# A hybrid attention and state-space layer on one core: more transposes done by VectorE and transfers, panels and lags in a new order

## The chip, the cores and the metric

The kernel runs on one core of a Trainium2 chip. Its time is device microseconds from the start to the end of one execution. Engines are named as in the profile: PE is TensorE, DVE is VectorE, ACT is ScalarE, POOL is GpSimd, SP is SyncE, which issues most of the loads.

## The reference

One layer on 256 tokens of width 1024, in float32, with nine outputs of one combined input projection:

```
h  = RMSNorm(x)
[q|k|v|z|xBC|dt|g_a|g_b] = h @ W_in
y_a = softmax attention(RMSNorm(q), RMSNorm(k), v) @ W_o_attn        16 heads of 64, causal
y_b = RMSNorm_groups(ssd(conv(xBC), dt) * silu(z)) @ W_o_ssm        32 heads of 64, 4 groups, chunks of 128
x   = x + (sigmoid(g_a) * y_a + sigmoid(g_b) * y_b) @ W_out
x   = x + (silu(h2 @ W_g) * (h2 @ W_u)) @ W_down,  h2 = RMSNorm(x)
x   = x + (p @ W_ple_proj) * sigmoid(RMSNorm(x) @ W_ple_gate)
```

With 256 tokens the attention has one block, so it is plain causal attention. All weights are read once from DRAM, about 100 MB with the inputs, and every product is float32.

## The kernel before

**Products in parts.** A float32 product is made of three fp32r ones: each weight tile of 128 x 1024 (`raw`) is rounded by ACT to a high part `wh`, DVE subtracts (`wl` = `raw` - `wh`), and TensorE adds `wh` x high, `wh` x low and `wl` x high of the activations. Loads are issued by SP in the order of use, through 4 buffers `raw` and 5 each of `wh` and `wl`. `load_tiles` has a branch for tile numbers in `BY_DMA` that makes the low part without DVE; the set is empty here:

```
act(tiles[2], tiles[0], scale=-1.0)
nc.gpsimd.dma_start(tiles[2], src[:, k : k + 2], accum_op=ALU.add)
```

**Panels.** The projections are made in panels of 512 output columns, in the order of the table `PANELS`; its entries name q, k, v, z, xbc, the gates ga and gb, and the output products ya (attention) and yb (state space). A panel in *token form* has tokens on the PSUM partitions, and one product is 48 matmuls of 512 columns. In *rows form* (xbc and z, function `by_rows`) channels are on the partitions, and a matmul has 256 columns (the tokens); a panel in `WIDE` puts high and low of the tokens side by side, so that 32 matmuls have 512 columns and 32 have 256. Panels live in 4 PSUM banks `g`; 4 more, `pb`, take everything else.

**Small work between the panels.** Transposes, scores, values and the state-space pieces are generators of a `Filler`. It keeps a planned time of TensorE (`fill.now`) and lets a generator go on when the number of nanoseconds that it asked for in the table `LAG` has passed. So `LAG` and `PANELS` fix the order of TensorE, and manual dependencies (`queue`, `follow`) hold it. The other engines' order is made by a scheduler at build time from priorities. Every engine runs its list in order.

**Two ways to transpose.** By TensorE: `transpose` against an identity into a `pb` bank (128 x 128 each), then ACT and DVE take the high and low part out of the bank (`evac_qk`, `split_pair`). By transfers ("moved"): `turn` is a DVE transpose of 32 x 32 blocks, `put` writes it to DRAM by one DMA per 128 tokens, `get` reads it back in the block order by four DMAs, and ACT and DVE split what arrives (`split_moved`). Put and get are issued by POOL. `Sent` is a put that leaves half by half. The sets `MOVED_*` say which tiles go this way: in the kernel before the half m of the merged output (`MOVED_M`), the residual after W_out (`MOVED_R`) and some others.

**Attention.** `evac_qk` squares a panel (ACT), sums per head (DVE, line 777), scales and adds epsilon (DVE, 778), takes the power -0.5 (POOL, 780), and scales the bank into SBUF (DVE, 781). Then q and k are transposed and split (820). `scores` makes two heads' scores into two banks, masks, exponentiates and normalises them; `transp` transposes the probabilities for `values`.

**State space.** For each pair of heads POOL writes masked sums (`rr`, line 872, affine selects), which TensorE sums into decays; `rstd_of` takes a power on POOL (512, 513) for the groups' norm.

**Tail.** After the MLP, `Residual.take` (line 1418) adds each half of w_down to the residual; the first half is moved, the second (n = 1) is transposed by TensorE in `split_pair`, split by ACT and DVE (1189), and multiplied with the last weights; `final` scales, multiplies, adds and stores (1569 to 1571).

Of the kernel before, what the change touches and what calls it, by code (L numbers as in the profile page):

```python
# [38 lines left out]
    ('gb', 1, 9760),  # L39
    ('xbc', 1, 5632),  # L40
    ('xbc', 5, 7680),
# [26 lines left out]
def by_rows():  # L68
# [4 lines left out]
WIDE = [('xbc', 0), ('xbc', 2), ('xbc', 3), ('xbc', 4), ('xbc', 5), ('z', 1), ('z', 2)]  # L73
# [18 lines left out]
    "dt.low": [322],
    "dt.end": [300],
    "c.get": [6000, 6000, 6000, 6000, 6000, 6000],
    "z.get": [6000, 6000, 6000, 6000],
    "x.get": [6000, 6000, 6000, 6000],
    "qk.get": [6000, 6000, 6000, 6000],
    "c.moved": [11500, 14000, 14000, 14000, 22000, 25400],
    "c.rows": [0, 2000, 0, 825, 500, 500],
    "x.moved": [28600, 8500, 20160, 14000],  # L100
    "x.start": [0, 0, 0, 0],
    "x.end": [5000, 4125, 2550, 1850],
    "p.moved": [24000, 15200, 20200, 8500, 24000, 8500, 24000, 24000],
    "qk.moved": [55800, 20000, 20000, 20000],
    "qk.split": [4200, 2560, 0, 4000],
    "xbc.end": [500, 0, 8000, 5175, 6606, 13539],
    "z.turn": [1000, 1000, 5000, 2000],
    "z.moved": [10000, 8500, 8500, 15000],
    "z.end": [0, 3383, 0, 10000],
    "qk": [14924, 21622, 13695, 19850],  # L110
    "qk.turn": [30000, 20000, 3500, 10000],
    "qk.t": [0, 500, 4448, 3521, 677, 1338, 1217, 1187],
    "qk.end": [0, 3102, 0, 3764],
    "v": [4043, 1000],
    "cb": [17, 0, 1060, 0],
    "rows": [4315],
    "prep": [5212, 300, 3707, 2704, 2974, 1163, 928, 2558],
    "seg": [4750, 2800, 500, 0, 0, 0, 1550, 4500, 300, 0, 2336, 1000, 3310, 4661, 1000, 2000],
    "seg.next": [10101, 11100, 0, 12046, 14480, 2104, 11572],
    "out": [0, 12163, 4964, 6250],  # L120
    "out.xdt": [0, 10000, 300, 0],
    "out.end": [509, 705, 4450, 0],
    "off": [1878, 3935, 0, 5814],
    "off.end": [0, 2831, 1117, 0],
# [64 lines left out]
def tile_layer(ctx: ExitStack, tc: tile.TileContext, head, xk, pt, vec, w_dt, w_big, w_dn2, w_pp, out):  # L189
# [1466 lines left out]
```

## Time and profile before

| | |
|---|---|
| median of 3 runs | 579.67 us (579.21 to 579.83) |
| profiled execution | 580.19 us, span 578.5 us |
| granted TensorE clock | 1.00 |
| busy: PE, DVE, ACT, POOL | 572.3, 443.0, 333.7, 82.0 us |
| DMA engines | 113.88 MB, mean 197 GB/s |

A busy PE row counts overlapping matmuls, so the rate of TensorE is read from the distance of starts, not from the mean duration. The chain of waits names, for each piece of time, the work that what followed had to wait for.

### The profile page before, as it was taken

The page shows a single profiled execution, that of the slowest core. Times are in us where ns is not written, and L with a number is a line of the kernel's source. Part 1 is how long each engine was busy: PE and PEld are TensorE (multiplying, and loading weights), DVE is VectorE, ACT ScalarE, POOL GpSimd, SP SyncE. Part 2 cuts the span into 40 slices and gives each one's busy share as a digit, 9 for nine tenths or more (in the row PEclk, how much of TensorE's full clock was granted, in tenths as well). Part 3 has the DMA queues.
Part 4 walks back from the last instruction along what each step waited for, and adds up shares of the span by engine and source line. Part 5 has one row for each costly group of instructions (what it writes and reads, how often), then busy time and mean ns, then how long its engine had stood idle before and what let it go on. Part 6 is the DMA issues. An engine that isn't in the chain of part 4 may idle for free.

```text
span 578.5 us, 8580 instructions
## 1 busy us (share of the span) xinstructions
PE 572.3 (99%) x3077; PEld 483.2 (84%) x3077; DVE 443.0 (77%) x696; ACT 333.7 (58%) x526; POOL 82.0 (14%) x116
## 2 busy tenths in 40 slices
PE   9999999999999999999999999999999999999996
PEld 8887898898988888888887888888888888888885
DVE  6668899998799899999757586776767767655563
ACT  6856567765668658666763544645455455444542
POOL 2011220000422310100000200300312012202010
PEclk9999999999999999999999999999999999999999
DMA  8874655545344653545445886576887687858611
GB/s 314 322 253 141 211 170 172 179 138 192 130 152 140 205 166 124 170 128 182 149 144 177 269 270 190 167 252 219 267 270 241 228 256 240 256 199 238 217 65 73
DMA packets 36458, 113.88 MB, mean 197 GB/s; under 512 B 4576, under 2 KB 8000, under 8 KB 36416
## 3 DMA queue, kind: packets, MB, share of 16 engines
q1 hardware_dynamic: 33088, 104.03, 54.7%
q0 software_dynamic: 3040, 8.92, 5.3%
q8 instruction: 24, 0.39, 0.3%
q10 hardware_dynamic: 288, 0.39, 0.2%
q14 instruction: 18, 0.15, 0.1%
HBM read 107.74 MB, written 5.52 MB: 196 GB/s over the span
## 4 chain that ended last, share of the span: by engine, by line
PE 88%; DMA 4%; DVE 4%; POOL 1%; ACT 1%; issue 1%; SPq 0%; ACTq 0%
PE g L273 78%; PE pb L273 8%; PE pb L295 3%; DMA raw<-in_w_big 2%; DVE wl L375 2%; DMA raw<-in_head 2%; POOL tiny L780 1%; ACT wh L252 1%; DVE s L1345 1%; DVE tiny L777 0%; DVE s L1347 0%; SPq L349 0%; ACT s L252 0%; DVE s L820 0%; DVE s L781 0%
## 5 line engine op out<-in xcount | busy, mean ns | idle before, releaser
L273 PE MATMUL g<-wh,s 128*128 128x512 f32 (+1 forms) x1156 | 358.9, 389 | 0.1
L252 ACT ACTIVATE wh<-raw 128x1024 fp32r<-128x1024 f32 (+2 forms) x192 | 199.0, 1040 | 177.7 <-PE g L273 137.3
L375 DVE TENSOR_TENSOR wl<-raw,wh 128x1024 fp32r<-128x1024 f32 (+2 forms) x193 | 230.9, 1199 | 90.0 <-ACT wh L252 88.4
L273 PEld LDWEIGHTS g<-wh,s 128*128 128x128 f32 x1156 | 216.3, 188 | 44.7 <-issue 0.5
L273 PE MATMUL g<-wl,s 128*128 128x512 f32 (+1 forms) x578 | 223.2, 388 | 0.0
L273 PEld LDWEIGHTS g<-wl,s 128*128 128x128 f32 x578 | 108.4, 188 | 21.9 <-issue 0.2
L273 PE MATMUL g<-s,wh 128*128 128x512 f32 (+1 forms) x416 | 114.5, 347 | 0.7 <-DVE s L781 0.7
L273 PE MATMUL g<-s,wl 128*128 128x256 f32 x320 | 86.6, 283 | 0.0
L273 PEld LDWEIGHTS g<-s,wh 128*128 128x128 f32 x416 | 70.6, 190 | 8.7 <-ACT wh L252 1.1
L273 PEld LDWEIGHTS g<-s,wl 128*128 128x128 f32 x320 | 60.6, 190 | 2.8
L252 ACT ACTIVATE s<-s 128x512 f32<-128x512 f32 (+4 forms) x45 | 35.0, 785 | 14.1 <-DVE s L1016 4.3
L252 ACT ACTIVATE s<-pb 128x512 f32<-128x512 f32 (+3 forms) x51 | 23.4, 477 | 14.8 <-PE pb L273 9.0
L273 PE MATMUL pb<-s,s 128*64 128x128 f32 (+5 forms) x336 | 29.0, 294 | 0.0
L872 POOL TENSOR_SCALAR_AFFINE_SELECT rr<-a_h 128x512 fp32r<-128x512 f32 x16 | 13.5, 863 | 108.7 <-PE pb L273 85.0
L273 PEld LDWEIGHTS pb<-s,s 128*64 128x64 f32 (+2 forms) x336 | 23.6, 158 | 5.9 <-issue 3.1
L780 POOL TENSOR_TENSOR tiny<-tiny,mhalf 128x8 f32<-128x8 f32 x8 | 19.7, 2461 | 48.2 <-DVE tiny L778 48.2
L647 DVE SCALAR_TENSOR_TENSOR s<-s,vecs,s 128x255 f32<-128x255 f32 (+2 forms) x60 | 26.3, 470 | 0.0
L749 POOL DMA_DIRECT2D s<-turn_d x36 | 19.8, 557 | 39.0 <-DMA turn_d<-s 36.9
L741 POOL DMA_DIRECT2D turn_d<-s x14 | 10.7, 762 | 100.3 <-DVE s L731 100.3
L252 ACT ACTIVATE s<-s,vecs 128x256 f32<-128x256 f32 (+1 forms) x44 | 21.7, 544 | 2.3 <-DVE s L1378 2.3
L295 PE MATMUL pb<-ident,s 128*128 128x128 f32 x146 | 22.1, 272 | 0.0
L252 ACT ACTIVATE s<-g 128x256 f32<-128x256 f32 (+1 forms) x46 | 20.3, 455 | 1.7 <-PE g L273 1.7
(145 smaller groups left out, 371.0 us busy)
## 6 DMA issues: line engine op xcount, KB each, us to landing
raw<-in_w_big SPq DMA_DIRECT2D x176, 512.0 KB
turn_d<-s POOLq DMA_DIRECT2D x16, 256.0 KB, 4.8
s<-turn_d POOLq DMA_DIRECT2D x32, 128.0 KB, 5.4
raw<-in_head SPq DMA_DIRECT2D x4, 512.0 KB
s<-in_xk SPq DMA_DIRECT2D x4, 512.0 KB
raw<-in_head SPq DMA_DIRECT2D x6, 256.0 KB
s<-e_d SPq DMA_DIRECT2D x8, 128.0 KB
raw<-in_w_pp SPq DMA_DIRECT2D x2, 512.0 KB
```

What stands on the lines that cost most here:

```text
L252: return nc.scalar.activation(o, i, f, **kw)
L273: ins = nc.tensor.matmul(o, lhsT, rhs, start=start, stop=stop).ins
L295: queue(nc.tensor.transpose(o, i, ident[: i.shape[0], : i.shape[0]]).ins, main)
L375: nc.vector.tensor_sub(wl, raw, wh.bitcast(F32))
L647: stt(cc[j][:, sft:], pu[:, j, : T - sft], cw[j][3 - sft], cc[j][:, sft:], op0=ALU.mult, op1=ALU.add)
L741: nc.gpsimd.dma_start(d[:, :, at : at + t_.shape[2]].rearrange("b p n -> p b n"), t_)
L749: nc.gpsimd.dma_start(o[32 * b : 32 * b + 32], d[b].rearrange("(a i) n -> i a n", i=32))
L780: nc.gpsimd.tensor_tensor(f, ms, mhalf, op=ALU.pow)
L872: nc.gpsimd.affine_select(r, bcast(a_h[:, c, h0 : h0 + 4].bitcast(F32), P), pattern=[[0, 4], [1, P]], compare_op=ALU.is_ge, fill=0.0, base ...
L1345: stt(h32[:, j], xk_, g1[:, k + j : k + j + 1], pr, op0=ALU.mult, op1=ALU.mult)
```

## The change

- `MOVED_QK = {0}`: q and k of the first half (k0, q0) go by `turn`, `put` and `get` instead of 16 transposes on TensorE.
- `MOVED_P`: the probabilities of three head pairs go the same way instead of 18 transposes; ACT scales them instead of DVE.
- `MOVED_Z = {2, 3}`: the panels z2 (was wide rows form) and z3 (was rows form) are made in token form and turned afterwards.
- `MOVED_E = {1}`: the residual of the tail, second half, goes by DVE and transfers instead of 8 transposes; its put and get are issued by SP.
- `BY_DMA = {38, 46, 54, 64}`: the low parts of four weight tiles are made by ACT and an accumulating DMA of POOL.
- `PANELS`: xbc5 ahead of xbc1, z2 ahead of xbc3, ga1 earlier, yb2 in two halves, and the last panel before w_out is the second half of yb3 instead of ya1.
- `LAG` and `FLIP`: all numbers new.

```diff
--- before.py
+++ after.py
@@ PANELS
     ('gb', 1, 9760),
+    ('xbc', 5, 7680),
     ('xbc', 1, 5632),
-    ('xbc', 5, 7680),
...
+    ('z', 2, 4096),
     ('xbc', 3, 6656),
-    ('z', 2, 4096),
     ('yb', 1, None),
     ('v', 1, 2560),
-    ('yb', 2, None),
+    ('ga', 1, 8736),
     ('ga', 0, 8224),
+    ('yb', 2, 0),
     ('yb', 3, 0),
     ('ya', 0, None),
-    ('ga', 1, 8736),
+    ('yb', 2, 1),
+    ('ya', 1, None),
     ('yb', 3, 1),
-    ('ya', 1, None),
...
-WIDE = [('xbc', 0), ('xbc', 2), ('xbc', 3), ('xbc', 4), ('xbc', 5), ('z', 1), ('z', 2)]
+WIDE = [('xbc', 0), ('xbc', 2), ('xbc', 3), ('xbc', 4), ('xbc', 5), ('z', 1)]
...
-    "m.moved": [22000],
+    "m.moved": [8500, 18300],
...
-MOVED_QK = set()
+MOVED_QK = {0}
 MOVED_X = set()
-MOVED_Z = set()
+MOVED_Z = {2, 3}
 MOVED_C = set()
-MOVED_P = set()
-BY_DMA = set()
+MOVED_P = {(1, 1), (1, 2), (1, 3)}
+BY_DMA = {38, 46, 54, 64}
 MOVED_M = {0}
+MOVED_E = {1}
...
-    def get(d):
+    def get(d, on=None):
 
         o = s4([4, d.shape[2]])
         for b in range(4):
-            nc.gpsimd.dma_start(o[32 * b : 32 * b + 32], d[b].rearrange("(a i) n -> i a n", i=32))
+            (on or nc.gpsimd).dma_start(o[32 * b : 32 * b + 32], d[b].rearrange("(a i) n -> i a n", i=32))
         return o
...
-        def __init__(self):
+        def __init__(self, on=None):
             self.d = dram.tile([4, P, T], F32, name=nm("turn_d"))
+            self.on = on or nc.gpsimd
...
-            turned = get(d).rearrange("p a (t i j) -> p i t a j", t=2, i=4)
+            turned = get(d, sent and sent.on).rearrange("p a (t i j) -> p i t a j", t=2, i=4)
...
-            sent = Sent() if self.normed and n == 0 else None
+            sent = Sent() if self.normed and n == 0 else Sent(nc.sync) if not self.normed and n in MOVED_E else None
...
+                elif sent:
+                    fill.spawn(split_moved([b[:, 0], b[:, 1]], self.cols(n), self.acts[n], lag("res"), sent), 0)
```

The tables do not show what moves. At three places it is this.

VectorE around the scaling of the first half's q and k (`s_99` is the first 128 tokens of q, `pb_600` and `pb_610` hold the transposed k). Before:

```order
L777 TENSOR_REDUCE tiny_563<-s_98_560 128x8
L820 SCALAR_TENSOR_TENSOR s_115_599<-pb_600,vecs,s_114_598 128x4x128
L820 SCALAR_TENSOR_TENSOR s_115_599<-pb_610,vecs,s_114_598 128x4x128
L778 TENSOR_SCALAR tiny_563<-tiny_563,eps_207 128x8
L375 TENSOR_TENSOR wl_779<-raw_777,wh_778 128x1024
L781 TENSOR_TENSOR s_99_561<-g_475,tiny_566 128x512
```

Now:

```order
L780 TENSOR_REDUCE tiny_563<-s_98_560 128x8
L781 TENSOR_SCALAR tiny_563<-tiny_563,eps_207 128x8
L377 TENSOR_TENSOR wl_760<-raw_758,wh_759 128x1024
L784 TENSOR_TENSOR s_99_561<-g_475,tiny_566 128x512
L580 TENSOR_REDUCE tiny_dt_596<-pb_595 128x64
```

The two splits of the transposed k are gone from between q's reduction and its scaling; the turns of both panels come later in VectorE's list.

POOL where the second half's q takes its powers, among the selects of the state space (`rr`), in the changed kernel, with the gets of a panel and the first accumulating DMA (`wl_1697`) ahead of them:

```order
L751 DMA s_184_1027<-turn_d_849 32x4x256 x4
L395 DMA wl_1697<-in_w_big 128x1024
L875 AFFINE_SELECT rr_1714<-a_h 128x512
L875 AFFINE_SELECT rr_1718<-a_h 128x512
L783 TENSOR_TENSOR tiny_1635<-tiny_1632,mhalf 128x8
L875 AFFINE_SELECT rr_2036<-a_h 128x512
L875 AFFINE_SELECT rr_2040<-a_h 128x512
L783 TENSOR_TENSOR tiny_1644<-tiny_1641,mhalf 128x8
```

Before, the two powers stood together behind eight selects:

```order
L872 AFFINE_SELECT rr_1794<-a_h 128x512
L872 AFFINE_SELECT rr_1798<-a_h 128x512
L872 AFFINE_SELECT rr_2088<-a_h 128x512
L872 AFFINE_SELECT rr_2092<-a_h 128x512
L780 TENSOR_TENSOR tiny_1686<-tiny_1683,mhalf 128x8
L780 TENSOR_TENSOR tiny_1695<-tiny_1692,mhalf 128x8
```

A pair of selects now stands between the two powers, and gets and an accumulating DMA ahead of them.

SP at the end of the program, where the last weights (`raw`) are loaded and the outputs stored. Before:

```order
L389 DMA raw_5587<-in_w_big 128x1024
L389 DMA raw_5593<-in_w_big 128x1024
L1571 DMA out<-s_1098_5577 128x512
L1571 DMA out<-s_1099_5582 128x512
L1571 DMA out<-s_1106_5635 128x512
```

Now:

```order
L391 DMA raw_5560<-in_w_big 128x1024
L391 DMA raw_5566<-in_w_big 128x1024
L761 DMA turn_d_5383<-s_1079_5385 128x4x128
L761 DMA turn_d_5383<-s_1080_5389 128x4x128
L751 DMA s_1098_5426<-turn_d_5383 32x4x256 x4
L1576 DMA out<-s_1113_5550 128x512
```

The two puts and four gets of the residual's second half stand between the last weight load and the first store, so they pass no load and only the stores stand behind them.

More of the change, by code (lines that the diff above doesn't have):

```diff
@@ L88 @@
 LAG = {
-    "dt": [8019],
-    "dt.t": [9610],
+    "dt": [7695],
+    "dt.t": [1649],
     "dt.e": [44376],
[L92 to L124, printed above, removed]
@@ L125 @@
-    "finish": [305, 9922, 13731, 6496],
-    "finish.ones": [10000, 2521, 0, 12856],
-    "sc": [8201, 2775, 5000, 0, 6165, 5667, 15876, 3962],
-    "sc.tr": [7150, 3550, 8766, 10000, 0, 680, 852, 0],
-    "tr": [0, 5000, 0, 0, 2688, 8460, 0, 739],
-    "tr.val": [8261, 5950, 21961, 0],
-    "val.end": [237],
-    "m": [3541, 0],
+    "dt.low": [1420],
+    "dt.end": [7330],
+    "c.get": [4600, 20580, 4500, 10000, 7500, 6618],
+    "z.get": [4500, 4500, 4884, 33641],
+    "x.get": [8244, 12274, 13232, 6932],
@@ new lines @@
+    "qk.get": [12918, 8033, 4500, 10000],
+    "c.moved": [34125, 31752, 10992, 30743, 8500, 32731],
+    "c.rows": [1000, 1200, 570, 1250, 675, 2749],
+    "x.moved": [13995, 8500, 47462, 23039],
+    "x.start": [2900, 300, 8000, 5000],
+    "x.end": [13264, 5000, 400, 1000],
+    "p.moved": [15262, 8500, 8500, 8500, 8500, 8500, 8500, 20319],
+    "qk.moved": [10248, 8500, 27777, 8500],
+    "qk.split": [0, 0, 5180, 9250],
+    "xbc.end": [4179, 10000, 1800, 6195, 1009, 27735],
+    "z.turn": [4786, 1000, 2000, 300],
@@ new lines @@
+    "z.moved": [21550, 8500, 15232, 12790],
+    "z.end": [1608, 2533, 166, 10000],
+    "qk": [35463, 4100, 10000, 500],
+    "qk.turn": [36000, 14085, 3250, 573],
+    "qk.t": [9888, 20340, 801, 2717, 7875, 1154, 500, 2000],
+    "qk.end": [6850, 5592, 6870, 6500],
+    "v": [500, 6762],
+    "cb": [5146, 300, 5500, 1180],
+    "rows": [32],
+    "prep": [360, 1220, 3538, 10000, 6191, 5850, 4616, 0],
+    "seg": [786, 1000, 1733, 2000, 0, 2240, 675, 2200, 270, 0, 4657, 630, 6561, 1161, 300, 300],
@@ new lines @@
+    "seg.next": [13430, 1807, 0, 10763, 3340, 13729, 1598],
+    "out": [0, 12126, 0, 1796],
+    "out.xdt": [23394, 6500, 9891, 4930],
+    "out.end": [0, 1900, 0, 4911],
+    "off": [4846, 6856, 5500, 500],
+    "off.end": [0, 4316, 0, 0],
+    "finish": [12156, 12574, 10000, 0],
+    "finish.ones": [10000, 4145, 0, 5360],
+    "sc": [3858, 9680, 4744, 9313, 6576, 2190, 10631, 2078],
+    "sc.tr": [49, 8107, 2493, 0, 0, 18653, 29052, 2020],
+    "tr": [540, 14500, 11511, 7222, 8494, 0, 2000, 2000],
@@ L133 @@
+    "tr.val": [0, 1100, 0, 0],
+    "val.end": [0],
+    "m": [8091, 716],
     "res": [5337, 5987],
-    "m.moved": [22000],
+    "m.moved": [8500, 18300],
     "r.moved": [24000],
@@ L151 @@
 FLIP = {
-    "sc": [1, 0, 1, 0, 1, 0, 1, 0],
-    "out": [0, 0, 1, 0],
-    "val": [1, 1, 0, 0],
+    "sc": [0, 1, 0, 1, 0, 0, 0, 1],
+    "out": [0, 1, 0, 1],
+    "val": [0, 1, 0, 0],
 }
@@ L1233, in joined @@
         acc, ga = accs[n], gates["ga", n]
-        sent = Sent() if n in MOVED_M else None
+        sent = Sent(nc.scalar if n else None) if n in MOVED_M else None
         with prio("ev"):
@@ L1243, in joined @@
         if sent:
-            fill.spawn(split_moved(toks, None, m_act[n], lag_of("m.moved", 0), sent), 0)
+            fill.spawn(split_moved(toks, None, m_act[n], lag_of("m.moved", n), sent), 0)
         else:
```

2 lines of the change are left out of this document (1 added, 1 removed).

## The prediction

> **What bounds the kernel now.** I read the shares of the engines first, then the chain of work that ended last, then the groups of TensorE's instructions by shape. The first row is the page's; the others are the chain in order of time (start us, length us, what).
>
> ```profile
> PE 572.3 (99%) x3077; PEld 483.2 (84%) x3077; DVE 443.0 (77%) x696; ACT 333.7 (58%) x526; POOL 82.0 (14%) x116
> ```
>
> ```profile
> 57.49 0.60 DVE tiny L777
> 58.08 0.07 DVE s L820
> ...
> 58.66 0.74 DVE s L820
> 59.40 0.15 DVE tiny L778
> ...
> 59.62 2.56 POOL tiny L780
> 62.20 0.70 DVE s L781
> ...
> 63.04 12.11 PE g L273 x98
> ...
> 345.52 0.44 PE pb L295 x4
> ...
> 401.36 156.75 PE g L273 x693
> ...
> 562.89 9.62 PE g L273 x48
> 572.51 1.45 PE pb L273 x12
> ```
>
> Up to 62.90 us the chain runs through loads, splits and one VectorE-GpSimd exchange; from 63.04 us it is TensorE alone, each piece starting where the one before it ends, until 573.96. So after 63 us an instruction taken from TensorE is worth its whole pitch, as long as no new wait opens. DVE, ACT and POOL have room on average, so they matter only where something of theirs is due at a given moment.
>
> The pitch comes from the chain: 156.75 / 693 = 0.2262 us for a matmul of 512 columns, and 0.44 / 4 = 0.11 us for a 128x128 transpose. "Mean ns" of a group is longer, since matmuls overlap; it is not used. For the two other shapes I take TensorE's timeline, in which the distance of starts is the pitch:
>
> ```profile
> 69.10 0.28 PE L273 MATMUL g<-s,wl 128*128 128x256 f32 x1
> 69.22 0.40 PE L273 MATMUL g<-s,wh 128*128 128x256 f32 x2
> 69.46 0.28 PE L273 MATMUL g<-s,wl 128*128 128x256 f32 x1
> ...
> 100.57 0.40 PE L273 MATMUL g<-s,wh 128*128 128x512 f32 x1
> 100.81 0.28 PE L273 MATMUL g<-s,wl 128*128 128x256 f32 x1
> 100.92 0.40 PE L273 MATMUL g<-s,wh 128*128 128x512 f32 x1
> ```
>
> Three 256-column matmuls of the rows form take 0.36 us (69.10 to 69.46), 0.12 each; one wide pair of 512 and 256 takes 0.35 (100.57 to 100.92).
>
> **What TensorE loses.** The instruction lists differ by 42 transposes: 16 of q and k, 18 of three pairs of probabilities, 8 of the last residual's second half. 42 x 0.11 = **-4.6 us**. They stand among these:
>
> ```profile
> L295 PE MATMUL pb<-ident,s 128*128 128x128 f32 x146 | 22.1, 272 | 0.0
> ```
>
> z2 goes from 32 wide pairs to 48 matmuls of 512 columns: 32 x 0.35 = 11.2, 48 x 0.2262 = 10.9, so -0.3. z3 goes from 96 of 256 columns to the same 48: 11.5 - 10.9 = -0.7. Together **-1.0 us**. The other matmuls keep shape and number; reordered panels cost nothing by themselves.
>
> **The place before 63 us.** The chain's VectorE rows show two L820 operations (the low parts of k of the first half) between the reduction L777 and L778. They are gone there, and with them their 1.3 us (58.08 to 59.40). TensorE's own last start before its gap is this:
>
> ```profile
> 61.95 0.39 PE L273 MATMUL g<-wh,s 128*128 128x512 f32 x1
> ```
>
> One pitch later, at 62.18, it would have gone on; it starts at 63.04, so it stands 0.86. In the new order 8 transposes ahead of it are away (already counted), so it arrives at 61.3, and the power, now 1.3 earlier, has L781 done at 61.6 and TensorE started at about 61.75. The gap shrinks to 0.45: **-0.4 us**. At best it closes (-0.9), at worst another DVE operation fills the hole (0).
>
> **The exchanges, and what hides them.** Each moved tile costs VectorE a turn, GpSimd (or SP) a put and four gets, and two landings:
>
> ```profile
> L731 DVE STREAM_TRANSPOSE s<-s 128x512 f32<-128x512 f32 x16 | 11.2, 705 | 0.3
> ...
> L820 DVE SCALAR_TENSOR_TENSOR s<-pb,vecs,s 128x512 fp32r<-128x512 f32 x8 | 5.8, 739 | 0.0
> ```
>
> ```profile
> L749 POOL DMA_DIRECT2D s<-turn_d x36: 549/553/624, 324.4 to 531.2; - x36
> L741 POOL DMA_DIRECT2D turn_d<-s x14: 755/758/823, 403.8 to 523.5; - x14
> ...
> DMA to landing us min/median/max: 2.7/4.9/7.1
> ```
>
> POOL (GpSimd) gets 46 DMAs more, 14 puts x 0.76 + 28 gets x 0.55 + 4 accumulating loads priced like puts = 29.1 us on an engine of 82.0; VectorE gets 16 turns (about 10 us) and loses 4 L375 and 4 L820 and multiplications, about as much. Neither fills up. What counts is latency: put, landing, get, landing is 2 x 4.9 plus about 3 of issue, some 13 us. I laid the new order of TensorE on the clock with the pitches above and compared when each result is used. k and q of the first half arrive 10 us or more before the scores that read them; the probabilities of the third moved pair some 3 us before their values; m of the first half, whose gets were issued in this way,
>
> ```profile
> 314.93 0.98 POOL L758 DMA_DIRECT2D turn_d<-s  x1 [26.92 <-DVE s L731]
> 319.54 0.76 POOL L758 DMA_DIRECT2D turn_d<-s  x1 [3.62 <-DVE s L731]
> 324.36 2.20 POOL L749 DMA_DIRECT2D s<-turn_d  x4 [4.06 <-DMA turn_d<-s]
> ```
>
> is now due 21.8 us after its last panel instead of 27, and needs about 17: still 4 spare. These I cost at nothing; cover gone, each costs what its landing exceeds the spare by.
>
> Two places are tight. The power L780 for q of the second half now stands on GpSimd behind selects that wait for TensorE's own segment sums, so q's scaling is about 1 us later, while the panel's bank is wanted soon after: 0 to 1.4 us, I take **+0.4**. And m of the second half, by TensorE's transposes as before (those at 345.52), is used about 8 matmuls earlier: its low part takes one ACT and one DVE step, due after 0.5 to 1 us, 0 to 0.4, I take **+0.2**.
>
> **The tail.** Residual n=1 is turned and goes out and back on SP's queue instead of by 8 transposes.
>
> ```profile
> 550.51 1.28 DVE L1418 TENSOR_TENSOR s<-g,s 128x512 f32<-128x512 f32 x2
> ...
> 558.59 1.64 ACT L252 ACTIVATE s<-pb,vecs 128x256 fp32r<-128x256 f32 x4 [1.04 <-PE pb L295]
> ```
>
> ```profile
> 550.62 0.33 SPq L389 DMA_DIRECT2D raw<-in_w_big  x1
> 567.90 7.83 SPq L1571 DMA_DIRECT2D out<-s  x5
> ```
>
> In the clock of before the additions end at 551.79, two turns at 553.2, the second put is issued by 553.6. SP waits there for it, then issues four gets (0.33 each), with nothing queued behind but the outputs. TensorE wants the first result at 562.89 - 0.88 = 562.0. No row has this exchange on SP's queue. From above: the median landing of GpSimd's transfers, twice: 553.6 + 4.9 + 1.3 + 4.9 = 564.7, plus 0.5 for ACT's split: a stall of 3.2. From below: 2.7 twice gives 560.8: none. The stage is nearest to the lower end, since the traffic has thinned:
>
> ```profile
> 115.00:160.00 45.00, 45.00 (x325) 41.40 (x324) 38.09 (x79) 28.34 (x59) 7.09 (x6) 1.00 0.47 153
> ...
> 400.00:550.00 150.00, 150.00 (x663) 124.20 (x663) 100.13 (x110) 73.06 (x81) 26.00 (x42) 1.00 0.76 239
> 550.00:578.00 28.00, 23.94 (x133) 20.73 (x131) 14.13 (x21) 10.05 (x17) 2.26 (x6) 1.00 0.19 67
> ```
>
> The last columns are the DMA engines' share and GB/s: 0.19 instead of 0.76. I take landings of 3.2, ready at 561.8, and a DVE low part a little late: **+0.4**. ACT holds the last weight's rounding behind these splits, but TensorE reaches that weight 30 matmuls (6.8 us) later.
>
> [...]
>
> **Low parts by DMA.** For four weight tiles ACT writes the negated rounding and an accumulating DMA adds the weights. No row shows such a DMA. Its nearest row is the four gets above, also 512 KB together on GpSimd's queue: landing between 2.7 and 7.1 after issue. TensorE wants those low parts 6 to 8 us after the issue, so I cost it at 0; four times a landing at the upper end plus 1 would be a few us.
>
> **The sum.** The profiled execution took 580.19 us, of which the span is 578.5; the median is 579.67, 0.5 lower. -4.6 - 1.0 - 0.4 + 0.4 + 0.2 + 0.4 = -5.0, and 0.3 for small waits that I did not find: -4.7. 580.2 - 4.7 - 0.5 = **575.0 us**. With all bounds at their good ends it is 573.2, with the two tight places and the tail at their bad ends about 579.
>
> **Rivals.**
>
> *The tail waits.* With median landings the stall of 3.2 replaces 0.4: 577.8. For it: 4.9 is what a transfer of this trace usually took, and the last weights' loads still run beside the puts. Against: 0.19 traffic. Chance 0.12.
>
> *GpSimd's single file.* A get waits on GpSimd for its put's landing, and powers and selects that TensorE needs stand behind it. L780 shows how such a wait is passed on: VectorE idled 8.8 us ahead of its eight scalings for it.
>
> ```profile
> L781 DVE TENSOR_TENSOR s<-g,tiny 128x512 f32<-128x512 f32 x8 | 5.5, 691 | 8.8 <-POOL tiny L780 8.8
> ```
>
> ```profile
> POOL rr L872 <- PE pb L273: 85.0, 6, 64.8
> ...
> POOL s L749 <- DMA turn_d<-s: 36.9, 8, 5.3
> ```
>
> GpSimd stood 36.9 / 8 = 4.6 us per exchange, and there are seven new ones on GpSimd, the early ones among the selects. If three of them pass on 1.4 us each, 575.0 + 4.2 = 579.2: no change. Against: GpSimd now waits 85.0 us for TensorE at its selects, so it is mostly early there. Chance 0.12. [...]
>
> *The accumulating DMAs land late; slower.* They must read the tile, add and write it. If that takes twice the gets' median of 4.9, 9.8 us, against 7 of cover, each of four holds TensorE 2.8 us, in order: +11.2, 586. From a landing of 8.5 (1.5 late, 4 x 1.5 = 6) the kernel is slower than before. Against: the maximum of 7.1, and the moderate traffic where the first of them stands (0.47 at 115 to 160 us). Chance 0.10.
>
> **How the numbers follow.** The forecast's case (573.2 to 577) has 0.66, the rivals 0.12, 0.12, 0.10. The range, 573.3 to 579.6, takes in the first two rivals and leaves out the slower one and a tenth of no-change cases. A measurement of this kernel tells a change of 0.2%, 1.2 us, from none: faster (below 578.5) is the first two cases and a third of the single-file case, 0.81; same 0.08; slower 0.11.
>
> **What would show it.** TensorE's L295 group at 104 instead of 146, its span's gap near 62 us at half a microsecond, no gap over 0.3 us between 63 us and the tail, and DMA landings of about 3 us on the tail's exchange. A wait of TensorE on the low parts written by DMA, or on a select behind a get, would make the prediction wrong; so would a lower granted clock than the 1.00 in the windows above.

## The result, and the profile after

The changed kernel takes **576.08 us** (median of 6 runs, 575.73 to 576.63) against 579.77 us of the kernel before on the same chip: ratio 0.9932, interval 0.9919 to 0.9945. That is 3.7 us less; the forecast was 4.7 less (575.0). The profiled execution took 576.59 us, its span 574.9 instead of 578.5; the granted clock was 1.00 in the windows up to TensorE's tail, so the prediction's proviso on the clock did not come in.

First the shares and the group of transposes of the kernel after, from the page and from the groups by shape:

```profile
PE 568.3 (99%) x2971; PEld 475.8 (83%) x2971; DVE 443.3 (77%) x703; ACT 337.8 (59%) x531; POOL 109.7 (19%) x162
...
L297 PE MATMUL pb<-ident,s 128*128 128x128 f32 x104 | 15.2, 272 | 0.0
```

TensorE has 106 matmuls less and is as full as before. VectorE's busy time hardly moved, GpSimd's rose by 27.7 us (29.1 forecast). The chain of waits of the kernel after, as start, length, work:

```profile
58.77 13.11 PE g L275 x71
...
90.55 0.34 DVE s L1381
...
90.93 27.31 PE g L275 x179
...
549.43 4.53 DMA turn_d<-s
...
555.43 2.87 DMA s<-turn_d
...
558.96 9.92 PE g L275 x48
568.88 1.45 PE pb L275 x12
```

Before, one piece of TensorE followed another from 63.04 us to the end. Now the chain leaves TensorE twice: from 72 to 91 us it runs over VectorE (a chain that is followed back lists all that VectorE did without a pause, so these 19 us are not 19 us of waiting), and in the tail it runs over the new exchange. What TensorE lost there is seen in its timeline, in which the distance of two starts is compared with the usual pitch. The three places of the kernel after (start us, length us, instruction; in brackets idle time and what ended it):

```profile
61.61 0.39 PE L275 MATMUL g<-wh,s 128*128 128x512 f32 x1
61.84 0.44 PE L275 MATMUL g<-s,wh 128*128 128x512 f32 x1
...
90.06 0.39 PE L275 MATMUL g<-s,wh 128*128 128x512 f32 x1
90.93 0.50 PE L275 MATMUL g<-s,wh 128*128 128x512 f32 x1 [0.48 <-DVE s L1381]
...
558.13 0.28 PE L275 MATMUL pb<-wh,s 128*128 128x256 f32 x1
558.96 0.50 PE L275 MATMUL g<-wh,s 128*128 128x512 f32 x1 [0.56 <-ACT s L254]
```

At 61.61 there is no gap in this profile, where before 0.86 us were lost. At 90.06 the distance is 0.87 instead of 0.24: 0.63 us lost, at a place that had no gap before. At 558.13 it is 0.83 instead of 0.12, and the first matmul behind it takes 0.11 longer (558.96 to 559.30): 0.82 lost.

A fourth loss is spread over a few matmuls. m of the second half is still transposed by TensorE, and the matmuls that read it follow haltingly:

```profile
350.31 0.40 PE L275 MATMUL g<-wl,s 128*128 128x512 f32 x1
350.70 0.74 PE L275 MATMUL g<-wh,s 128*128 128x512 f32 x2
351.28 0.40 PE L275 MATMUL g<-wl,s 128*128 128x512 f32 x1
```

0.39 instead of 0.227, then 0.58 instead of 0.454 for two; with the matmul before and after them 0.44 us.

TensorE's last matmul ends at 570.33 instead of 573.96, 3.63 us earlier. By places, against the terms of the prediction:

| place | predicted us | measured us |
|---|---|---|
| 42 transposes | -4.6 | -4.58 |
| z2, z3 in token form | -1.0 | -0.98 |
| near 62 us | -0.4 | -0.32 |
| q1's power behind selects | +0.4 | 0 |
| m, second half | +0.2 | +0.44 |
| tail exchange | +0.4 | +0.82 |
| 90 us (L1381) | not listed | +0.63 |
| small waits | +0.3 | +0.36 (the rest) |
| sum | -4.7 | -3.63 |

The first two rows are not measured at a place: they are the counts, which the groups confirm, times the usual distance of starts of each shape. The row near 62 us is 63.04 - 61.84 = 1.20, less the 8 transposes ahead of it (0.88), which the first row has. The table compares one profile of each kernel, and the experiments show that two of its rows, near 62 us and the tail, change by several tenths of a microsecond from one profile to the next, even of the same instructions.

### The profile page after: what moved, and what is told of

Its sections match the earlier page's. It is cut to its first block, busy times and chain, and to the rows that moved or that the text cites. A ratio compares the mean times of both kernels' runs of the same rounds, so it can differ in the third digit from the quotient of the medians.

```text
span 574.9 us, 8489 instructions
## 1 busy us (share of the span) xinstructions
PE 568.3 (99%) x2971; PEld 475.8 (83%) x2971; DVE 443.3 (77%) x703; ACT 337.8 (59%) x531; POOL 109.7 (19%) x162
## 4 chain that ended last, share of the span: by engine, by line
PE 93%; DVE 3%; DMA 2%; issue 1%; ACT 1%; SPq 0%; ACTq 0%; DVEq 0%
PE g L275 83%; PE pb L275 8%; PE pb L297 2%; DVE s L649 1%; DVE wl L377 1%; DMA turn_d<-s 1%; DMA raw<-in_head 1%; DMA s<-turn_d 0%; ACT wh L254 0%; ACT s L254 0%; SPq L751 0%; DVE s L1421 0%; DVE s L1381 0%; DVE s L656 0%; DVE tiny_dt L596 0%
## 5 line engine op out<-in xcount | busy, mean ns | idle before, releaser
L275 PE MATMUL g<-wh,s 128*128 128x512 f32 (+1 forms) x1220 | 382.3, 391 | 0.7 <-ACT s L254 0.6
L275 PEld LDWEIGHTS g<-wh,s 128*128 128x128 f32 x1220 | 228.8, 189 | 49.1 <-ACT s L254 1.5
L275 PE MATMUL g<-wl,s 128*128 128x512 f32 (+1 forms) x610 | 235.7, 388 | 0.0
L275 PE MATMUL g<-s,wh 128*128 128x512 f32 (+1 forms) x320 | 91.0, 354 | 0.5 <-DVE s L1381 0.5
L275 PE MATMUL g<-s,wl 128*128 128x256 f32 x256 | 68.8, 283 | 0.0
L275 PEld LDWEIGHTS g<-s,wh 128*128 128x128 f32 x320 | 54.8, 188 | 7.7 <-DVE s L1381 1.0
L275 PEld LDWEIGHTS g<-s,wl 128*128 128x128 f32 x256 | 48.3, 189 | 2.0 <-issue 0.2
L751 POOL DMA_DIRECT2D s<-turn_d x64 | 35.3, 558 | 55.2 <-DMA turn_d<-s 41.1
L875 POOL TENSOR_SCALAR_AFFINE_SELECT rr<-a_h 128x512 fp32r<-128x512 f32 x16 | 13.4, 851 | 59.9 <-PE pb L275 46.7
L733 DVE STREAM_TRANSPOSE s<-s 128x512 f32<-128x512 f32 (+2 forms) x34 | 21.8, 657 | 1.3 <-ACT s L254 0.9
L254 ACT ACTIVATE s<-s,tiny 128x128 f32<-128x128 f32 (+1 forms) x44 | 18.6, 446 | 6.1 <-DVE tiny L1075 5.8
```

What stands on the lines that cost most here:

```text
L254: return nc.scalar.activation(o, i, f, **kw)
L275: ins = nc.tensor.matmul(o, lhsT, rhs, start=start, stop=stop).ins
L733: nc.vector.transpose(t_.rearrange("p b (x j) -> p x b j", j=32), src.rearrange(f"p {dims[1]} -> p x b j", b=4, j=32))
L751: (on or nc.gpsimd).dma_start(o[32 * b : 32 * b + 32], d[b].rearrange("(a i) n -> i a n", i=32))
L875: nc.gpsimd.affine_select(r, bcast(a_h[:, c, h0 : h0 + 4].bitcast(F32), P), pattern=[[0, 4], [1, P]], compare_op=ALU.is_ge, fill=0.0, base ...
```

## The experiments

Each kernel below is the changed kernel with one edit, unless the text says otherwise. Times are medians; ratios are against the kernel before on the same chip.

**The tail taken back.** Only `MOVED_E` is emptied, so the residual's second half goes by 8 transposes again.

```diff
-MOVED_E = {1}
+MOVED_E = set()
```

> The changed kernel with the last residual's second half transposed by TensorE again (8 transposes). Theory, from the trace after: the exchange on SP's queue made TensorE wait about 0.8 us, 8 transposes cost 0.88, so moving it won nothing: 576.1 us, within 0.3, no TensorE gap over 0.3 us in the last 40 us. Rival, as the prediction had it (most of the 0.88 was won): 576.6 to 577.0.

Measured: 576.68 us (576.45 to 577.19), ratio 0.9937 (0.9922 to 0.9953). The median is 0.6 above the changed kernel's, but the two ratios are not told apart, and in the profiles the difference does not come from the tail. From the 600th-last matmul that is not a transpose to the last one TensorE took 131.67 us here, 131.65 with the exchange, and 131.67 in the kernel before. The 0.88 us of transposes and the 0.82 of the wait cancel: **in these two profiles the move in the tail won nothing.** TensorE's order over this stretch is the same in every kernel of this document but for the 8 transposes, so their profiles can be compared too. Without the exchange they take 131.66 or 131.67 us (three kernels). With it on SP's queue the changed kernel and eight of its variants take 130.79 to 131.65, in the middle 131.31, though the two puts are issued at the same point of the stretch in all nine. From the second put's issue to the first get it is 4.68 us in the changed kernel's profile, 4.14 in that with later turns and 3.55 in that with q and k taken back; in the last two the stretch takes 130.85 and 130.79, and TensorE does not wait at all. So the wait goes from nothing to 0.8 us, the changed kernel's profile has the longest of the nine, and in the middle one the move won about 0.35 us. The difference between the two profiles compared first lies near 62 us, in this kernel's TensorE timeline:

```profile
61.10 0.39 PE L275 MATMUL g<-wh,s 128*128 128x512 f32 x1
62.13 0.47 PE L275 MATMUL g<-s,wh 128*128 128x512 f32 x1 [0.65 <-DVE s L784]
```

TensorE is half a microsecond earlier at this place than in the changed kernel's profile (61.10, not 61.61) and then waits for VectorE's scaling L784. It goes on at 62.13 instead of 61.84, from a program that is the same up to the tail. So this place alone differs by 0.3 us between the two profiles. Two more pairs of profiles with the same instructions up to the tail bear this out: with the tail on GpSimd's queue TensorE goes on at 61.73, and in the kernel before it does so at 63.04, but at 62.58 when only the tail is changed. Less the 0.88 of the transposes, that is 61.70 to 62.16 against 61.73 to 62.13: **a gain near 62 us isn't shown**; the -0.32 is that of one pair of profiles.

**The tail alone.** The kernel before with only the tail exchange; TensorE's order is otherwise that of before.

```diff
 MOVED_M = {0}
+MOVED_E = {1}
 MOVED_R = {0}
...
+                elif sent:
+                    fill.spawn(split_moved([b[:, 0], b[:, 1]], self.cols(n), self.acts[n], lag("res"), sent), 0)
```

> The kernel before with one part of the change, the tail's exchange on SP's queue (8 transposes less); the lists of all engines are the same up to the last panels. Theory, from the trace after (8 transposes 0.88 us, TensorE's wait 0.7 to 0.8 us): no change, 579.6 to 580.0 where the kernel before has 579.9. Rival, as the prediction had it: 0.5 us faster. Rival, median landings of 4.9 us twice: 2 us slower.

Measured: 579.99 us against 580.27, ratio 0.9996 (0.9983 to 1.0008): no change that the runs can tell, but the interval, -1.0 to +0.5 us, leaves room for a gain of half a microsecond. Its tail:

```profile
561.19 0.28 PE L274 MATMUL pb<-wh,s 128*128 128x256 f32 x1
562.41 0.50 PE L274 MATMUL g<-wh,s 128*128 128x512 f32 x1 [0.95 <-ACT s L253]
```

The wait is 1.22 - 0.12 = 1.1 us, somewhat more than the 0.88 that it replaces (stretch 132.01 instead of 131.67). It is the longest tail of all profiles with the exchange on SP's queue.

**The tail on GpSimd's queue.** Put and get are issued by POOL instead of SP.

```diff
-Sent(nc.sync) if not self.normed and n in MOVED_E
+Sent() if not self.normed and n in MOVED_E
```

> The changed kernel with the tail's put and get issued by POOL instead of SP. Theory (the landing of the put, 4.5 us in the trace, comes from the weight loads beside it and is the same from any queue; POOL only issues slower, 0.76 against 0.38 per put and 0.55 against 0.42 per get): TensorE waits 0.9 us longer, 577.0 us. Rival (POOL's transfers have a longer way of their own, 4.8 and 5.4 us to land): 578.5 or more.

Measured: 577.03 us (576.98 to 578.14), ratio 0.9937 (0.9919 to 0.9956). In its trace the wait is 1.05 (558.05 to 559.09) instead of 0.83, and the stretch is 0.20 us longer. The median is the 577.0 that was expected, but on a chip where the kernel before takes 580.27, and the ratio is not told apart from the changed kernel's 0.9932. In the traces the queue is worth 0.2 us, less than the tail varies between profiles on SP's queue; so what the queue is worth stays open.

**No accumulating DMAs.** The four low parts are VectorE's again.

```diff
-BY_DMA = {38, 46, 54, 64}
+BY_DMA = set()
```

> The changed kernel with the four low parts made by VectorE again. Theory: the accumulating DMAs (8.2 to 9.2 us to land) are hidden and VectorE has room after 100 us, so nothing changes: 576.1 us, within 0.3. Rival one: VectorE's 4 x 1.2 us come back as waits of TensorE between 120 and 235 us: 577 or more. Rival two: the 2 MB of extra reads and the late landings cost something that the gaps do not show: below 575.7.

Measured: 583.43 us (582.58 to 584.64), ratio 1.0054 (1.0033 to 1.0074): slower than the kernel before. I had expected next to nothing; the first rival, VectorE's work coming back as waits of TensorE between 120 and 235 us, was right. TensorE's and GpSimd's timelines of this kernel:

```profile
150.41 0.40 PE L275 MATMUL g<-wh,s 128*128 128x512 f32 x1
151.31 0.47 PE L275 MATMUL pb<-rr,gt_r 128*128 128x512 f32 x1 [0.50 <-issue]
```

```profile
148.76 1.66 POOL L783 TENSOR_TENSOR tiny<-tiny,mhalf 128x8 f32<-128x8 f32 x1 [3.21 <-DVE tiny L781]
150.42 3.88 POOL L875 TENSOR_SCALAR_AFFINE_SELECT rr<-a_h 128x512 fp32r<-128x512 f32 x4
```

This is the tight place of the prediction, q1's powers among GpSimd's selects. GpSimd's timeline of the changed kernel at the same place:

```profile
147.83 1.66 POOL L783 TENSOR_TENSOR tiny<-tiny,mhalf 128x8 f32<-128x8 f32 x1 [2.79 <-DVE tiny L781]
149.47 1.22 POOL L875 TENSOR_SCALAR_AFFINE_SELECT rr<-a_h 128x512 fp32r<-128x512 f32 x2
```

Without the DMAs VectorE has one subtraction of 1.2 us more up to here (seven instead of six from 121 us on), stands idle for 1.07 us at 142.8 behind ACT's rounding, and hands its L781 over 0.9 us later. The power starts at 148.76 instead of 147.83, GpSimd's list now has four selects behind it instead of two, and TensorE's next matmul is a segment sum, which reads the selects' results. The view names no releaser for this wait (`issue`); that the sum waits for the first select is read from the times. Three more waits of 2.1, 2.0 and 0.9 us follow at 154.42, 173.49 and 211.28. The changed kernel has no wait of TensorE at this place. So the accumulating DMAs hold nothing up, and without them VectorE is late here.

**q and k taken back.**

```diff
-MOVED_QK = {0}
+MOVED_QK = set()
```

> The changed kernel with q and k of the first half transposed by TensorE again (16 transposes, 1.76 us). Theory A: the gap near 62 us closed because this tile was moved, so both come back: 1.76 + 0.86 = 578.7 us. Theory B: it closed because the new lags place the splits behind the scaling, so the gap stays shut and only the transposes return: 577.8 us. In both, if the four turns were what made VectorE late at 90 us, that gap of 0.6 goes and the time is 0.6 lower.

Measured: 591.33 us (590.65 to 592.86), ratio 1.0197 (1.0173 to 1.0222), 15 us above the changed kernel, where 16 transposes are worth 1.8. Both expectations were far too low. The largest loss of this kernel:

```profile
111.22 0.39 PE L275 MATMUL g<-s,wh 128*128 128x512 f32 x1
115.20 1.65 PE L275 MATMUL pb<-s,s 128*128 128x256 f32 x4 [3.59 <-DVE s L656]
```

L656 ends one step of the convolution on VectorE. It is done at 115.15 here and at 114.58 in the changed kernel, so VectorE did not fall back. But the product that reads it stands at 118.08 in the changed kernel's TensorE order and at 111.46 in this one. The lags were chosen for another set of generators; with q and k back among TensorE's pieces they let this product go 6.6 us earlier, ahead of its data. The wait is followed by some 6 us of work at half the clock (below), and by waits of 2.0, 1.4 and 1.0 us at 207.91, 248.48 and 325.48.

**The probabilities taken back.**

```diff
-MOVED_P = {(1, 1), (1, 2), (1, 3)}
+MOVED_P = set()
```

> The changed kernel with the three pairs of probabilities transposed by TensorE again (18 transposes, 2.0 us; VectorE scales them again). Theory A, parts add up: 578.1 us, with the groups of transposes as the only difference on TensorE. Theory B, the table of lags holds only for this set of moved tiles, and each part taken out shifts VectorE's and POOL's lists so that TensorE waits: 580 or more, with new gaps.

Measured: 579.02 us (577.73 to 580.59), ratio 0.9977 (0.9964 to 0.9990): 2.9 above the changed kernel. 18 transposes are 2.0; in the profiled execution about one more stands near 62 us (a distance of 1.42). There VectorE's scaling starts only at 62.48. This part alone behaves roughly as a sum would have it.

**z2 and z3 taken back.** z2 is again wide, z3 again in rows form.

```diff
-WIDE = [('xbc', 0), ('xbc', 2), ('xbc', 3), ('xbc', 4), ('xbc', 5), ('z', 1)]
+WIDE = [('xbc', 0), ('xbc', 2), ('xbc', 3), ('xbc', 4), ('xbc', 5), ('z', 1), ('z', 2)]
...
-MOVED_Z = {2, 3}
+MOVED_Z = set()
```

> The changed kernel with z2 and z3 in rows form again (z2 wide). Theory A, parts add up: their 1.0 us of matmul pitch returns, 577.1 us. Theory B: new waits of TensorE on VectorE, 579 or more.

Measured: 584.05 us (581.81 to 586.08), ratio 1.0075 (1.0059 to 1.0091), 8 us above the changed kernel instead of 1. The profiled execution took 581.81, the shortest of the eight, so some 2 us of the median are not in it. One wait of 3.3 us stands at 203.65, where transposes wait for the scaling L784 of a panel, and that for its power on GpSimd:

```profile
202.40 3.72 POOL L783 TENSOR_TENSOR tiny<-tiny,mhalf 128x8 f32<-128x8 f32 x1 [9.05 <-DVE tiny L781]
```

This panel's first power took 1.67 in the changed kernel (at 195.70). In the kernel before it took 3.68 (at 196.91), and TensorE did not wait for it there.

**The new tables without the moves.** All sets as before, `PANELS`, `LAG` and `FLIP` new.

```diff
...
-MOVED_QK = {0}
+MOVED_QK = set()
...
-MOVED_Z = {2, 3}
+MOVED_Z = set()
...
-MOVED_P = {(1, 1), (1, 2), (1, 3)}
-BY_DMA = {38, 46, 54, 64}
+MOVED_P = set()
+BY_DMA = set()
...
-MOVED_E = {1}
+MOVED_E = set()
```

> The changed kernel's order of panels and lags with nothing more moved than in the kernel before (all 42 transposes on TensorE, z2 and z3 in rows form, no accumulating DMA). Theory A, parts add up: 576.1 + 4.6 + 1.0 + what else the order itself gives or takes, 581 to 582 us. Theory B, order and moves belong together: 585 or more, with waits of several us. Rival: the order alone is the gain: below 579.

Measured: 592.52 us (592.21 to 592.84), ratio 1.0213 (1.0186 to 1.0241). The same wait for L656 as with q and k taken back, 3.98 us at 112.16; 2.1 us at 211.31; and, at 92.97, a gap like the changed kernel's at 90.06:

```profile
92.97 0.40 PE L275 MATMUL g<-s,wh 128*128 128x512 f32 x1
94.03 0.50 PE L275 MATMUL g<-s,wh 128*128 128x512 f32 x1 [0.66 <-DVE s L1381]
```

**The moves with the old tables.** The changed kernel with `PANELS`, `LAG` and `FLIP` of before.

```diff
-    ('xbc', 5, 7680),
     ('xbc', 1, 5632),
+    ('xbc', 5, 7680),
...
-    "dt": [7695],
-    "dt.t": [1649],
+    "dt": [8019],
+    "dt.t": [9610],
```

> The changed kernel's moved tiles (42 transposes less, token form of z2 and z3, four accumulating DMAs) with the order of panels and the lags of the kernel before. Theory A, parts add up and the order by itself is worth little: 575 to 577 us. Theory B, moves and order belong together: 582 or more, with waits of several us.

Measured: 599.1 us (598.9 to 599.3), ratio 1.0313 (1.0286 to 1.0339), the slowest of all. The values of a moved pair wait for their exchange:

```profile
313.04 0.39 PE L274 MATMUL g<-wh,s 128*128 128x512 f32 x1
324.35 1.98 PE L274 MATMUL pb<-s,s 128*64 128x256 f32 x10 [10.92 <-DMA s<-turn_d]
```

Another wait, of 3.6 us, stands at 150.90. Behind the two, TensorE worked at half its clock (granted clock 0.59 from 154 to 158 us and 0.98 from 158 to 162; 0.50 from 324 to 328 and from 328 to 332), some 11 us together, which by my estimate from these windows is 5 to 6 us of the loss.

So the moves alone cost some 19 us, the tables alone 12, and both together win 3.7. With these numbers none of the two is worth anything without the other. In neither kernel were the lags fitted anew, so what the moves could win with lags of their own in the old order of panels isn't shown. Near 90 us this kernel has no gap; one of 0.76 us, also behind the evacuation of a wide panel (line 1380 here), stands at 106.63.

**The gap at 90 us.** Here TensorE waits for L1381, the evacuation of a wide panel, for its bank. VectorE's list ahead of it, in the changed kernel:

```profile
88.06 1.25 DVE L649 SCALAR_TENSOR_TENSOR s<-g,vecs,s 128x253 f32<-128x253 f32 x3
89.23 1.21 DVE L377 TENSOR_TENSOR wl<-raw,wh 128x1024 fp32r<-128x1024 f32 x1
...
90.47 0.41 DVE L1381 TENSOR_TENSOR s<-g,s 128x256 f32<-128x256 f32 x1
```

VectorE works without a pause, and the convolution and a weight's low part stand ahead of L1381. I tried three edits. The first moves the four turns of q and k of the first half out of the stretch by later lags.

```diff
-    "qk.get": [12918, 8033, 4500, 10000],
+    "qk.get": [5000, 5000, 4500, 10000],
...
-    "qk.moved": [10248, 8500, 27777, 8500],
+    "qk.moved": [5000, 5000, 27777, 8500],
...
-    "qk.turn": [36000, 14085, 3250, 573],
+    "qk.turn": [52000, 38000, 3250, 573],
```

> The changed kernel with the four turns of the first half's q and k held back until VectorE's crowded stretch from 72 to 91 us is over (lags alone). Theory: their 2.8 us in that stretch are what TensorE waits for at 90 us, so the gap of 0.6 us goes: 575.4 us. Rival one: the wait comes from the order of the two panels (the wide one first) whatever else VectorE does: gap and time stay, 576.1. Rival two: the exchange is then too late for the scores near 117 us: a new gap there, 576.5 or more.

Measured: 582.01 us (579.73 to 584.33), ratio 1.0034 (1.0018 to 1.0050). The edit went wrong: the turns came out directly ahead of L1381.

```profile
91.01 2.48 DVE L733 STREAM_TRANSPOSE s<-s 128x512 f32<-128x512 f32 x4
...
94.91 0.42 DVE L1381 TENSOR_TENSOR s<-g,s 128x256 f32<-128x256 f32 x1
```

The gap there grew from 0.87 to 3.58 us (at 91.80). What stands ahead of L1381 in VectorE's list is paid by TensorE in full; whether less in the stretch before it would close the gap, this run doesn't tell.

The second gives VectorE one subtraction less, by a fifth accumulating DMA for a weight of this stretch.

```diff
-BY_DMA = {38, 46, 54, 64}
+BY_DMA = {22, 38, 46, 54, 64}
```

> The changed kernel with a fifth low part made by the accumulating DMA: that of the tile which VectorE splits at 80.8 us, in the stretch from 72 to 91 us in which it is never idle. Theory (VectorE's list ahead of the evacuation at 90.5 us is what TensorE waits for there): 1.2 us less in it, the gap of 0.6 us closes, 575.4 us. Rival: the low part lands 8.2 to 9.2 us after its issue and TensorE waits for it instead: a new gap near 85 us of 1 to 5 us, 577 or more.

Measured: 582.79 us (581.12 to 584.44), ratio 1.0052 (1.0034 to 1.0069). The gap stayed (1.42 us at 89.37). VectorE was idle for 0.64 us at 81.7, waiting for a weight's rounding, and L1381 came at 90.33 as ever. A subtraction less did not bring L1381 forward. New waits arose at 154.44 (2.07 us) and 165.76 (0.81).

The third puts the evacuation ahead in VectorE's list, by a higher priority.

```diff
-                        with prio("ev"):
+                        with prio("hot"):
                             act(u[:, j], ps[:, T:])
                             nc.vector.tensor_add(u[:, j], ps[:, :T], u[:, j])
```

> The changed kernel with one word changed: the evacuation of the wide panels (ACT's copy and VectorE's addition L1381) gets the first rank, so that it stands ahead of the next weight's low part in VectorE's list. Theory (the gap at 90 us is the evacuation standing behind a weight's low part and four convolution steps, not VectorE's total load): L1381 runs about 1.2 us earlier there, the gap of 0.6 us closes, 575.4 us. Rival one (VectorE has no slack in that stretch): the delay moves to the next low part, which TensorE then waits for, 576.1. Rival two: low parts come late elsewhere, 577 or more.

Measured: 577.59 us (575.89 to 579.45), ratio 0.9941 (0.9920 to 0.9961): not told apart from the changed kernel. L1381 does stand ahead of the subtraction now, but in the profiled execution ACT waited for a weight's load, and VectorE, in order behind ACT, stood idle for 2.35 us:

```profile
84.41 1.06 ACT L254 ACTIVATE wh<-raw 128x1024 fp32r<-128x1024 f32 x1 [4.55 <-DMA raw<-in_w_big]
```

L1381 came at 91.48, and the gap at 89.81 was 2.13 us.

This load was late where the DMA engines are full (their share was 0.91 from 78 to 82 us and 1.03 from 82 to 86 in this profile). The changed kernel's window (busy time of PE, PEld, DVE, ACT, POOL, then granted clock, DMA share and GB/s) shows the same traffic, and the kernel with the new tables and no moves shows what it is without q's and k's exchanges, here second:

```profile
78.00:82.00 4.00, 4.00 (x35) 4.00 (x34) 4.00 (x9) 1.31 (x3) 0.00 (x0) 1.00 0.95 225
```

```profile
78.00:82.00 4.00, 4.00 (x36) 4.00 (x35) 4.00 (x10) 2.02 (x4) 0.00 (x0) 1.00 0.44 153
```

I had suspected this traffic as the cause of the gap. It is not: with the new tables and a DMA share of 0.44 the distance is 1.06 us (92.97), and with q and k taken back, so also without their exchanges, 1.08 (92.02). With all moves and the old tables there is none near 90 us, nor in the kernel before. **The gap at 90 us comes with the new order of the panels and lags**, not with the exchanges. Whether full DMA engines make it longer, as the 2.13 us in the third edit's profile would have it, was not shown. Which line of the tables makes it I did not try: xbc5 now comes ahead of xbc1 there, and no run here moves this pair alone.

No experiment gave a kernel that beats the changed one.

## Why the prediction was right, and where it was off

**The core was right.** TensorE bounds the kernel from 63 us on, and an instruction taken from it is priced at its pitch: -4.58 for 42 transposes at 0.109 each, -0.98 for the two panels. These 5.56 us carry the result, and the distances of starts, not the mean durations, gave them. They were not measured one by one; what bears them out is that with the waits seen at their places the sum leaves a rest of 0.36 us.

**Near 62 us**, "the gap shrinks to 0.45: -0.4 us": measured -0.32. The gap itself is gone (a gap of half a microsecond was what the prediction asked to see), but that is partly because in this execution TensorE started slowly. The kernels' first matmuls, before and after:

```profile
4.31 1.68 PE L273 MATMUL g<-wh,s 128*128 128x256 f32 x8
```

```profile
4.30 2.14 PE L275 MATMUL g<-wh,s 128*128 128x256 f32 x8
```

The same eight matmuls took 2.14 us instead of 1.68; the changed kernel's TensorE lost 0.46 us there and came to this place at 61.61, when VectorE's scaling L784 (60.97 to 61.66) was all but done. In the profiles of the other kernels with the new tables the scaling starts between 59.9 and 61.3, and at 62.48 with the probabilities taken back. TensorE goes on at 61.21 to 61.34 where it is early (three kernels, among them those without accumulating DMAs and without z) and at 62.13 and 63.32 where VectorE is late (the tail and the probabilities taken back). The mechanism is there, since the two splits of k are gone, but its size is not: the instructions of the kernel before, too, go on at 63.04 in one profile and at 62.58 in another, and so the -0.4 is neither borne out nor refuted.

**The tail**, "I take landings of 3.2, ready at 561.8 ... +0.4": in the changed kernel's profile the wait was twice that, +0.82. The put took 4.53 us (549.43 to 553.96) and the get 2.87, 7.4 together instead of 6.4. The step that failed is "the stage is nearest to the lower end, since the traffic has thinned": the 0.19 was a mean over 28 us, and the second put left at 549.43, only 2.1 us after the issue of the last weight load (up to 547.35). The changed kernel's window:

```profile
550.00:552.00 2.00, 2.00 (x11) 1.65 (x10) 1.25 (x2) 1.06 (x1) 1.83 (x4) 1.00 0.87 252
```

With a DMA share of 0.87 there the put was hardly faster than a median transfer (4.8); from 552 us to 554 the share was 0.10. Over the ten profiles with this exchange on SP's queue the wait goes from nothing to 1.1 us, with about 0.5 in the middle, so the +0.4 was a fair middle, reached by a wrong reading of the traffic, and its lower bound, no wait, is what two kernels show. In these two the share under the put was as high (0.92 and 0.88 over 2 us), so the traffic alone doesn't explain the spread, and its cause stays open. The first rival, a stall of 3.2, was wrong.

**"These I cost at nothing"**: the exchanges of q, k, m and the probabilities opened no wait, as said. q1's power, +0.4, cost nothing either in the changed kernel; but it is a real edge, since without the accumulating DMAs TensorE waits there. The second half of m cost +0.44, at the bad end of its bounds (0 to 0.4).

**The accumulating DMAs**, "landing between 2.7 and 7.1 after issue. TensorE wants those low parts 6 to 8 us after the issue, so I cost it at 0": the result was right and both numbers were wrong. The lookup of this DMA's issues in the trace after says:

```profile
L395 POOL DMA_DIRECT2D wl<-in_w_big x4: 916/952/982, 129.8 to 227.0; - x4
...
DMA to landing us min/median/max: 8.2/8.8/9.2
```

They land after 8.2 to 9.2 us, far above 4.9 and near the 9.8 of the slower rival. With 7 us of cover this would have cost 4 x 1.8 = 7 us. But the cover was larger. The last one is issued and first used here:

```profile
226.96 0.97 POOL L395 DMA_DIRECT2D wl<-in_w_big  x1
```

```profile
237.84 0.48 PE L275 MATMUL g<-wl,s 128*128 128x512 f32 x1
```

10.9 us; the other three have 12.6 to 15.1. The rival failed on its cover, not on its price, and in my own step two errors cancelled.

**"Reordered panels cost nothing by themselves"** is the step that was plainly wrong. The new order, of panels and lags together, cost 0.63 us at 90 us, where TensorE waits for L1381 and VectorE's list ahead of it is another one. "Neither fills up" was a statement about averages (DVE 77%), and over 70 to 94 us VectorE is busy all the time, before and after (23.90 and 24.00 of 24 us). I had looked for results that come late by transfer, and not for an evacuation that stands late in an engine's list. The prediction's own sign, no gap over 0.3 us between 63 us and the tail, was not met here.

**GpSimd's single file**, the second rival, does not show in the changed kernel; it shows as soon as a part is taken out (without the DMAs at 150 us, without z at 203 us). That VectorE's work and the queue were in balance only with the whole set was in none of my cases. I had added up the parts. One part (the probabilities) can be taken out at its own price; the others cost 7 (accumulating DMAs), 8 (z) and 15 us (q and k) when taken out, instead of 0 to 1.8.

The sum of what was off, in the two profiles of the table: q1 -0.4, m +0.24, tail +0.42, 90 us +0.63, near 62 us +0.08, small waits +0.06, together +1.0, which is the distance from -4.7 to -3.63.

## What to carry to other kernels

Where one engine has no idle time, price a removed instruction by the distance of its starts, and then go through the other engines' lists at each place where the order changes, asking what now stands ahead of each evacuation, not only whether the engine has room on average. Where an order was fitted by lags, the parts of a change don't add up: taking one part back tells what the fitted set loses without it, not what the part is worth. A transpose taken out just ahead of the place where its result is needed wins only what the exchange's two landings leave over (4.53 and 2.87 us in the changed kernel's tail, where 0.88 us of transposes were taken out and TensorE waited 0.82), so read the traffic in the few microseconds of the put itself, not as a mean of the stage, and compare several profiles before a wait of half a microsecond is called a result.

## What the runs showed of the hardware

**TensorE's clock after a wait.** After waits of 3.58 us and more TensorE ran at half its rate for some microseconds. Waits are given here as distances of starts, and how long the half rate lasted is worked out from the granted clock of the windows: later turns, wait 3.58, some 3.4 us; old tables, wait 3.59, some 3.4; q and k taken back and the new tables alone, wait 4.0 for L656, some 6.9; old tables, wait 11.3, 8 or more (324 to 332 us). The kernel with q and k taken back, windows behind its wait at 111.22 (the granted clock is the third number from the right):

```profile
111.00:115.00 4.00, 0.61 (x4) 0.29 (x2) 3.33 (x3) 2.00 (x2) 0.00 (x0) 0.92 0.68 224
115.00:119.00 4.00, 3.80 (x18) 3.01 (x19) 1.93 (x8) 1.86 (x7) 0.00 (x0) 0.50 0.49 157
```

In the next window, 119 to 123 us, the clock is 0.72: half the rate up to about 121.2, some 6.9 us in all. With the new tables alone it is 0.82, 0.50 and 0.82 from 112 to 124 us. With later turns, after a wait of 3.58 us at 91.80, the distance from a matmul of 512 columns to the next start was 0.43 (96.18 to 96.61) instead of 0.24, for some 3.4 us (granted clock 0.62 from 94 to 98 us, 0.95 from 98 to 102). The wait of 3.34 us without z2 and z3 (203.65) did not do this in its profile (granted clock 1.00 from 203 to 215 us); but the other seven runs of that kernel were all longer, and in six of them the granted clock was 0.994 to 0.996 instead of 0.998, so it may have done it there. The changed kernel's waits at 90.06 (a distance of 0.87) and 558.13 (0.83) did not do it (1.00 from 90 to 98 us and from 550 to 568). A wait of 2.08 us did it, at 154.42 without accumulating DMAs (0.91 from 154 to 158 us, 0.66 from 158 to 162), and it seems one of 2.07 at 154.44 with five, where the clock of the whole execution is 0.995 against the changed kernel's 0.998. Four others near 2 us did not: 2.00 at 173.49 without accumulating DMAs (1.00 from 173 to 181), 2.04 at 207.91 with q and k taken back (1.00 from 209 to 217), and 2.13 with the evacuation ahead (0.999 for the whole execution) and with the new tables alone (0.992, which the 6.9 us above and the changed kernel's 0.998 account for). Behind the 2.08 at 154.42 came twelve short matmuls on half the array (64 * 128), and full ones only 3.9 us after the wait's start (158.30). Behind the wait at 111.22 came 13 short matmuls up to 118 us, nine of them on half the array, and the half rate lasted twice as long as after the wait at 91.80, which full ones followed at once (95.38). What decides it, no run tells.

**GpSimd beside VectorE.** In the tail of the changed kernel a short GpSimd operation lasts until VectorE's subtraction ends. GpSimd's timeline, then VectorE's:

```profile
551.46 1.07 POOL L514 TENSOR_SCALAR tiny<-tiny 128x1 f32<-128x1 f32 x1
```

```profile
551.26 1.23 DVE L377 TENSOR_TENSOR wl<-raw,wh 128x1024 fp32r<-128x1024 f32 x1 [0.75 <-ACT wh L254]
```

The subtraction ends at 552.49, the GpSimd operation at 552.53, and the pair ahead of them (VectorE 549.33 to 550.51, GpSimd 549.43 to 550.56) does the same. Where no subtraction is beside it, the operation takes 0.19 us (at 367.80 in the changed kernel, at 553.46 and 554.54 in the kernel before). In these rows GpSimd is the one that waits: the two subtractions take 1.18 and 1.23 us, the mean of their group 1.19. The issues of its gets take 549 to 624 ns, beside such subtractions too (550 to 569 for the 37 of 64 that overlap one). The power of 3.72 us at 202.40, in the kernel with z2 and z3 taken back, fits these rows. Beside it VectorE does this there:

```profile
202.23 1.22 DVE L1019 TENSOR_TENSOR s<-s,s 128x1024 f32<-128x1024 f32 x1
203.36 1.22 DVE L377 TENSOR_TENSOR wl<-raw,wh 128x1024 fp32r<-128x1024 f32 x1
```

Two instructions that read two tiles each, from 202.40 to 204.58, are 2.18 us; with 1.66 for the power alone (147.83 in the changed kernel) that is an estimate of 3.84, about what it took. No run takes these two away, but the eight powers of the kernel before fit as well: the five that start 0.15 to 0.21 us after a subtraction take 2.50 to 2.58 us, and the two with none under way take 1.64; one with a second such instruction behind the subtraction takes 3.68.
